# A hybrid attention and ConvGLU block: three more column pairs by seven products, remainders of the pair sums by accumulating transfers, and the row of 1/rms by way of DRAM

## The chip, the cores and the metric

One core of a Trainium2 chip runs the whole kernel. Its engines run side by side, each in its own order: TensorE (PE in the profile, its weight loads PEld), VectorE (DVE), ScalarE (ACT), GpSimd (POOL) and SyncE (SP). SP and POOL issue nearly all DMA transfers here, each from a queue that it works through in order. The metric is the device time of one execution in microseconds.

## The reference

One transformer-like layer on x of 512 rows (tokens) by 1024 columns, all in float32:

```
h    = rms_norm(x, norm1_g);  proj = h @ w_in          # q, k, v of branches A and B, gates gA, gB
yA   = chunked softmax attention(qA, kA, vA) @ w_branch_a
yB   = stick-breaking attention(qB, kB, vB) @ w_branch_b
x    = x + (sigmoid(gA) * yA + sigmoid(gB) * yB) @ w_out
hid  = rms_norm(x, norm2_g) @ w_ffn_up                 # 1024 -> 2 * 2816
gate, up = causal depthwise conv of width 3 (hid) + bias
x    = x + (silu(gate) * up) @ w_ffn_down              # 2816 -> 1024
```

rms_norm divides a row by the root of its mean square, so 1/rms is one number per token.

## The kernel before

Every float32 product is made of three products in the faster fp32r format. A matrix is split into hi (the value rounded to fp32r, a copy on ACT) and lo (value minus hi, a subtraction on DVE), and hi·hi, hi·lo and lo·hi are added up in PSUM.

The weights stream through in chunks. A chunk is loaded into one of two `raw` tiles by SP, split while TensorE works on the chunk before (`split_gen`), and then multiplied (`run_chunk`). The order of chunks is a fixed list: qA0, kA0, vA0, qA1, kA1, vA1, gA0, vB0, gA1, ..., then the output projections, then `up0` to `up21`, then the down projection in two sweeps of eleven chunks, `dn0_0` to `dn0_10` and `dn1_0` to `dn1_10`. Attention steps run between the chunks of the first half. A scheduler fixes the final order of the instructions on every engine when the program is built.

**The row of 1/rms.** 1/rms of the first norm is made as a column (one number per partition, `rstd`, in the tile `cols`). The gates gA and gB and the keys kB are computed with tokens along the free axis, so they need 1/rms as a row that is the same in all partitions, `rrow`. `norm1_row` makes it with four small TensorE products of `rstd` with the identity into a PSUM bank and a copy of that bank on ACT (L351 to L358). Its users are L514 (gA), L498 (kB) and L544 (gB).

**An up chunk** `up{j}` holds 128 columns of the gate and 128 of the up half. An ordinary one (`up_body`) takes two products of 8 x 3 matmuls with 512 columns. The chunks in the list `SEVEN` use Strassen's scheme of seven half-size products instead of eight: `up_seven` has seven products of 4 x 3 matmuls with 256 columns (L998), over sums of blocks of the weights (`block_sums`, tile `sx`, with their split in `wxh` and `wxl`) and over sums of blocks of the input (`token_sums`, four tiles with tag `ts`). Its results are put together on ACT and DVE in `pc`, `hg` and `hu`. After the products, `conv` applies the three taps (one ACT and two DVE instructions for each half), ACT takes the silu in the one buffer `cg`, and DVE multiplies into a slot of `ub`, which has four.

**A pair** is two neighbouring chunks, after odd j. The down projection uses a seven-product scheme as well, so `pair_sums` makes sums of blocks of the two results (tile `st`, one buffer) and splits them into hi and lo: `ax` (four blocks, used in the first sweep) and `ay` (three blocks, used in the second). `halves` does the split: a copy on ACT (L908) and a subtraction on DVE (L909) for each of four pieces of 768, 256, 256 and 512 columns. There are eight buffers with tag `ax` and one `ay`, so `ay` of pairs 0 to 6 is written to the DRAM tensor `ayd` by a DMA on POOL (L933), and `fetch` brings it back later (L953), into tiles that are free by then: the first five after `up18`, two more in the first down sweep. Pair 8 has its `ax` in a `ts` tile and its `ay` in `wxh`.

## Time and profile before

| | us |
|---|---|
| median of 3 runs | 726.53 (726.07 to 726.63) |
| the profiled execution | 726.66 |
| its span in the trace | 724.9 |
| TensorE busy in the span | 718.6 (99%) |
| VectorE busy | 565.4 (78%) |
| ScalarE busy | 401.5 (55%) |
| GpSimd busy | 53.6 (7%) |

The span reaches from the first to the last instruction; 1.8 us of the execution lie around it. The granted TensorE clock is 1.00 throughout. GpSimd's busy time leaves out the DMA issues, which its queue also holds.

### The profile page before, as it was taken

The numbers are of one execution on the slowest core, as the hardware profiler recorded it, in microseconds if no ns is written. First come the engines' busy times: TensorE is split into PE (matmuls) and PEld (weight loads), VectorE is DVE, ScalarE is ACT, GpSimd is POOL, SyncE is SP. The second block draws the span as 40 slices with busy tenths as digits, with TensorE's granted clock in tenths as the row PEclk, the third lists the DMA queues.
The fourth block names the chain that finished last, engine by engine and source line by source line (L and its number), as shares of the span: only waits on it lengthen the run. The fifth ranks groups of instructions, "written<-read, shape, count | busy, mean of one in ns | idle before, by whom it ended". The sixth has DMA issues, their size and how long they took to land.

```text
span 724.9 us, 10589 instructions
## 1 busy us (share of the span) xinstructions
PE 718.6 (99%) x4019; PEld 627.5 (87%) x4019; DVE 565.4 (78%) x1030; ACT 401.5 (55%) x727; POOL 53.6 (7%) x95
## 2 busy tenths in 40 slices
PE   8999999999999999999999999999999999999997
PEld 8999998888988888888889889889898988888886
DVE  6678867775988888566275799998979985997686
ACT  6675656657767676442254556655545653543541
POOL 2701200000101011000012000000000100000000
PEclk9999999999999999999999999999999999999999
DMA  8632232211313111314536613544335553564563
GB/s 308 250 131 78 83 117 74 74 59 58 118 63 113 59 59 59 136 68 144 195 149 239 203 62 156 186 135 160 118 145 186 181 184 117 173 243 174 177 222 116
DMA packets 24786, 100.91 MB, mean 139 GB/s; under 512 B 2592, under 2 KB 7328, under 8 KB 17184
## 3 DMA queue, kind: packets, MB, share of 16 engines
q1 hardware_dynamic: 21792, 87.00, 33.8%
q0 software_dynamic: 2656, 13.11, 5.0%
q8 instruction: 31, 0.51, 0.3%
q14 instruction: 19, 0.16, 0.1%
q10 hardware_dynamic: 288, 0.14, 0.1%
HBM read 88.44 MB, written 11.80 MB: 138 GB/s over the span
## 4 chain that ended last, share of the span: by engine, by line
PE 98%; DMA 1%; SPq 0%; DVE 0%; ACT 0%; DVEq 0%; issue 0%
PE P L1087 14%; PE p L998 7%; PE pg L254 4%; PE pg L253 4%; PE pg L255 4%; PE pu L254 4%; PE pu L255 4%; PE pu L253 4%; PE qkB L255 2%; PE gB L255 2%; PE qkB L253 2%; PE gA L253 2%; PE gA L254 2%; PE gB L253 2%; PE gA L255 2%; PE qkB L254 2%
## 5 line engine op out<-in xcount | busy, mean ns | idle before, releaser
L253 PE MATMUL pg<-hth,whi_up 128*128 128x512 f32 (+1 forms) x152 | 55.7, 367 | 0.0
L255 PE MATMUL pg<-hth,wlo_up 128*128 128x512 f32 (+1 forms) x152 | 55.7, 366 | 0.0
L254 PE MATMUL pg<-htl,whi_up 128*128 128x512 f32 (+1 forms) x152 | 55.7, 366 | 0.0
L254 PE MATMUL pu<-htl,whi_up 128*128 128x512 f32 (+1 forms) x152 | 55.6, 366 | 0.0
L253 PE MATMUL pu<-hth,whi_up 128*128 128x512 f32 (+1 forms) x152 | 55.6, 366 | 0.0
L255 PE MATMUL pu<-hth,wlo_up 128*128 128x512 f32 (+1 forms) x152 | 55.6, 365 | 0.0
L1087 PE MATMUL P<-whi_dn,ax 128*128 128x512 f32 x176 | 54.4, 389 | 0.0
L149 ACT CAST whi_dn<-raw_dn 128x1024 fp32r<-128x1024 f32 x33 | 34.3, 1051 | 25.5 <-PE P L1087 15.2
L145 DVE TENSOR_TENSOR wlo_dn<-raw_dn,whi_dn 128x1024 fp32r<-128x1024 f32 x33 | 40.0, 1224 | 9.2 <-ACT whi_dn L149 9.1
L228 DVE TENSOR_TENSOR wlo_up<-raw_up,whi_up 128x1024 fp32r<-128x1024 f32 (+1 forms) x40 | 41.2, 1062 | 7.0 <-ACT whi_up L226 7.0
L226 ACT CAST whi_up<-raw_up 128x1024 fp32r<-128x1024 f32 (+1 forms) x40 | 34.5, 917 | 14.7 <-PE pu L254 7.9
L1087 PE MATMUL P<-whi_dn,ay 128*128 128x512 f32 x132 | 40.8, 389 | 0.0
L1087 PEld LDWEIGHTS P<-whi_dn,ax 128*128 128x128 f32 x176 | 33.0, 188 | 6.8
L1087 PE MATMUL P<-wlo_dn,ax 128*128 128x512 f32 x88 | 34.2, 389 | 0.0
L254 PEld LDWEIGHTS pu<-htl,whi_up 128*128 128x128 f32 x152 | 28.6, 188 | 4.7
L253 PEld LDWEIGHTS pu<-hth,whi_up 128*128 128x128 f32 x152 | 28.5, 188 | 4.7
L255 PEld LDWEIGHTS pg<-hth,wlo_up 128*128 128x128 f32 x152 | 28.6, 188 | 4.7
L255 PEld LDWEIGHTS pu<-hth,wlo_up 128*128 128x128 f32 x152 | 28.5, 188 | 4.6
L253 PEld LDWEIGHTS pg<-hth,whi_up 128*128 128x128 f32 x152 | 28.6, 188 | 4.6
L254 PEld LDWEIGHTS pg<-htl,whi_up 128*128 128x128 f32 x152 | 28.6, 188 | 4.5
L633 DVE TENSOR_TENSOR_SCAN aB<-aB,reset 128x127 f32<-128x127 f32 (+3 forms) x32 | 26.0, 817 | 6.7 <-ACT aB L628 6.7
L1087 PEld LDWEIGHTS P<-whi_dn,ay 128*128 128x128 f32 x132 | 24.8, 188 | 5.1
(303 smaller groups left out, 2240.3 us busy)
## 6 DMA issues: line engine op xcount, KB each, us to landing
raw_up<-in_wts SPq DMA_DIRECT2D x22, 1024.0 KB, 4.8
raw_dn<-in_wd SPq DMA_DIRECT2D x11, 1024.0 KB, 4.8
raw_dn<-in_wd SPq DMA_DIRECT2D x11, 512.0 KB, 3.4
ayd<-ay POOLq DMA_DIRECT2D x7, 768.0 KB, 5.2
ay<-ayd POOLq DMA_DIRECT2D x7, 768.0 KB, 6.5
raw_gA<-in_wts SPq DMA_DIRECT2D x4, 1024.0 KB, 4.7
raw_qkB<-in_wts SPq DMA_DIRECT2D x4, 1024.0 KB, 4.8
raw_gB<-in_wts SPq DMA_DIRECT2D x4, 1024.0 KB, 4.7
```

Source lines behind the costliest of these rows:

```text
L145: chain("halves", V.tensor_tensor(o, x, y, op=op))
L149: chain("casts", A.copy(hi[:, sl], src))
L226: A.copy(hi[:, sl], raw[:, sl])
L228: E.tensor_tensor(lo[:, sl], raw[:, sl], hi[:, sl].bitcast(F32), op=ALU.subtract)
L253: PE.matmul(ps, sh, mh, start=first, stop=False)
L254: PE.matmul(ps, sh, ml, start=False, stop=False)
L255: PE.matmul(ps, sl, mh, start=False, stop=last)
L633: V.tensor_tensor_scan(ar, ar, reset[:, S - n:S - 1][:, ::-1], 1.0, op0=ALU.mult, op1=ALU.max)
L998: PE.matmul(ps, st, mv[:, k, :], start=first and k == 0 and n == 0, stop=last and k == 3 and n == 2, skip_group_check=True)
L1087: chain("products", PE.matmul(dst, st, mv, start=first and n == 0, stop=last and n == 2, skip_group_check=True))
```

## The change

- `SEVEN` grows from five chunks (5, 8, 11, 14, 17) to eight (5, 8, 10, 12, 14, 16, 18, 20), so that from up7 on every second chunk is of this kind.
- In `halves`, for pairs 0 to 8, lo is no longer a DVE subtraction. ACT writes minus the rounded value into lo (a second ACT instruction for each piece), and a DMA on POOL adds the value to it in place (`accum_op=ALU.add`). Pairs 9 and 10 keep the subtraction.
- Pair 8 gets an `ax` buffer and the `ay` buffer like the others. For this, `ay` of pair 7 is written to `ayd` too, and `ax` of pair 0 is written to a new DRAM tensor `axd` and fetched into a `ts` tile after `up20`.
- The fetches are emitted after `up20` (pairs 0 and 1) and after chosen down chunks (the others).
- `norm1_row` goes. SP writes `rstd` to a DRAM tensor `row` and later reads it back, spread over all partitions, into `rrow`; `behind(..., (late["ld"],))` places the write behind the load of vA1's weights in SP's queue, and the read behind that of vB0.

```diff
-SEVEN = (5, 8, 11, 14, 17)
+SEVEN = (5, 8, 10, 12, 14, 16, 18, 20)
...
-            SP.dma_start(raw[:, sl], wts[i, :, sl])
+            late["ld"] = SP.dma_start(raw[:, sl], wts[i, :, sl])
...
-    rrow = norm1_row()
     for s in range(len(steps)):
+        if s == 4:
+            behind(SP.dma_start(row.rearrange("t p -> p t"), rstd), (late["ld"],))
+        if s == 9:
+            behind(SP.dma_start(rrow, bass.AP(row.tensor, row.offset, [[0, P], [1, S]])), (late["ld"],))
...
                 A.copy(a[:, sl], src)
-                ins.append(V.tensor_tensor(a[:, n + o:n + sl.stop], src, a[:, sl].bitcast(F32), op=ALU.subtract))
+                if i < 9:
+                    A.activation(lo, src, AF.Copy, scale=-1.0)
+                    G.dma_start(lo, src, accum_op=ALU.add)
+                else:
+                    ins.append(V.tensor_tensor(lo, src, a[:, sl].bitcast(F32), op=ALU.subtract))
...
-            if j // 2 < 7:
+            if j // 2 < 8:
                 G.dma_start(ayd[j // 2], pairs[j // 2][1].bitcast(F32))
+            if j // 2 == 6:
+                G.dma_start(axd, pairs[0][0].bitcast(F32))
...
-        if j == 18:
-            for i in range(5):
+        if j == SEVEN[-1]:
+            keep[0] = fp.tile([P, S], F32, tag="hg", name="t2_0")
+            ax0 = fp.tile([P, 2048], F32R, tag="ts", name="ax0_", bufs=4)
+            G.dma_start(ax0, axd)
+            pairs[0] = (ax0, None)
+            for i in range(2):
                 fetch(i)
...
+            n = ({1: 2, 3: 6, 5: 7, 7: 3, 9: 4}, {0: 5})[s].get(i)
+            if n is not None:
+                fetch(n)
```

How the built order changes at the places that the prediction speaks of. First SP's queue in the first half, where `raw_` are weight loads and `tt` the bias tiles; before:

```order
L132 DMA raw_vA1_715<-in_wts 128x2048
L132 DMA raw_gA0_928<-in_wts 128x2048
L586 DMA tt2_880<-in_rbx 128x512
L586 DMA tt3_1132<-in_rbx 128x512
L132 DMA raw_vB0_1124<-in_wts 128x2048
L586 DMA tt4_1381<-in_rbx 128x512
```

and SP's queue at the same place now:

```order
L132 DMA raw_vA1_711<-in_wts 128x2048
L723 DMA row_192<-cols_191 128x4x1
L132 DMA raw_gA0_925<-in_wts 128x2048
L582 DMA tt2_877<-in_rbx 128x512
L582 DMA tt3_1130<-in_rbx 128x512
L132 DMA raw_vB0_1121<-in_wts 128x2048
L725 DMA rrow_193<-row_192 128x512
L582 DMA tt4_1379<-in_rbx 128x512
```

The two transfers stand where `behind` puts them; the loads around them keep their order.

Second, POOL's queue through the up chunks, from pair 3 to the fetches; before:

```order
L933 DMA ayd_108<-ay3_4972 128x1536
L933 DMA ayd_108<-ay4_5175 128x1536
L933 DMA ayd_108<-ay5_5383 128x1536
L953 DMA ay0_6036<-ayd_108 128x1536
L933 DMA ayd_108<-ay6_5544 128x1536
L953 DMA ay1_6038<-ayd_108 128x1536
```

and POOL's queue now, for one pair (pair 4, as for the others):

```order
L907 DMA ay4_5197<-ub_4182 128x256
L907 DMA ax4_5196<-st4_5198 128x256
L907 DMA ax4_5196<-ub_4182 128x768
L907 DMA ay4_5197<-st4_5198 128x512
L933 DMA ayd_108<-ay4_5197 128x1536
```

and now at the turn to the down projection, where one queue of fetches stands:

```order
L1061 DMA ax0__6389<-axd_109 128x2048
L956 DMA ay3_6790<-ayd_108 128x1536
L956 DMA ay4_6862<-ayd_108 128x1536
L956 DMA ay2_6557<-ayd_108 128x1536
L956 DMA ay1_6393<-ayd_108 128x1536
L956 DMA ay5_6935<-ayd_108 128x1536
```

Each write to `ayd` now stands behind four accumulating transfers and has to wait for the two into `ay`, and five fetches of `ay` stand together behind the one of `ax0_`.

Third, ACT from the end of up10 to the end of pair 4, now (L903 are the rounded copies, L906 the negated ones, L199 the split of up12, L850 the taps):

```order
L903 CAST ay4_5197<-ub_4182 128x256
L906 ACTIVATE ay4_5197<-ub_4182 128x256
L199 CAST wxh_up12_5354<-sx_up12_5271 128x512
L199 CAST whi_up12_5352<-raw_up12_5190 128x1024
L850 ACTIVATE cg10_5314<-hg10_5221,par_88 128x512
L199 CAST whi_up12_5352<-raw_up12_5190 128x1024
L903 CAST ax4_5196<-st4_5198 128x256
L906 ACTIVATE ax4_5196<-st4_5198 128x256
L903 CAST ax4_5196<-ub_4182 128x768
L906 ACTIVATE ax4_5196<-ub_4182 128x768
L850 ACTIVATE ub_4182<-hu10_5222,par_88 128x512
L903 CAST ay4_5197<-st4_5198 128x512
```

Here every rounded copy has a negated one right behind it; the negated copy of the last piece follows as the next row.

More of the change, by code (lines that the diff above doesn't have):

```diff
@@ L264, in block_kernel @@
     htd = dram.tile([NT, 2, P, S], F32, tag="htd", name="htd")
-    ayd = dram.tile([7, P, 1536], F32, tag="ayd", name="ayd")
+    ayd = dram.tile([8, P, 1536], F32, tag="ayd", name="ayd")
+    axd = dram.tile([P, 2048], F32, tag="axd", name="axd")
     reset = pool_c.tile([P, S], F32, tag="reset", name="reset")
@@ L349, in norm1 @@
         V.tensor_scalar_mul(nrstd[:, c], rstd[:, c], -1.0)
-    def norm1_row():
-        ps = PV("rrow")
-        for t in range(NT):
-            PE.matmul(ps[:, t * P:(t + 1) * P], rstd[:, t:t + 1].to_broadcast([P, P]), ident,
-                      start=True, stop=True)
-        r = pool_c.tile([P, S], F32, tag="rrow", name="rrow")
-        A.copy(r, ps)
-        return r
+    row = dram.tile([NT, P], F32, tag="row", name="row")
+    rrow = pool_c.tile([P, S], F32, tag="rrow", name="rrow")
     kg = par[:, C_KG:C_KG + 1]
@@ L875, in pair_sums @@
         t = {}
-        if i < 8:
+        if i < 9:
             ax = fp.tile([P, 2048], F32R, tag="ax", name=f"ax{i}", bufs=8)
             ay = fp.tile([P, 1536], F32R, tag="ay", name=f"ay{i}")
-        elif i == 8:
-            ax = fp.tile([P, 2048], F32R, tag="ts", name=f"ax{i}", bufs=4)
-            ay = fp.tile([P, 1600], F32R, tag="wxh", name=f"ay{i}")[:, 0:1536]
-            keep[0] = fp.tile([P, S], F32, tag="hg", name="t2_0")
         else:
@@ L907, in halves @@
                 sl = slice(o, o + src.shape[-1])
+                lo = a[:, n + o:n + sl.stop]
                 A.copy(a[:, sl], src)
-                ins.append(V.tensor_tensor(a[:, n + o:n + sl.stop], src, a[:, sl].bitcast(F32), op=ALU.subtract))
+                if i < 9:
+                    A.activation(lo, src, AF.Copy, scale=-1.0)
+                    G.dma_start(lo, src, accum_op=ALU.add)
+                else:
+                    ins.append(V.tensor_tensor(lo, src, a[:, sl].bitcast(F32), op=ALU.subtract))
             return ins
@@ L948, in fetch @@
     def fetch(i):
-        tag = {0: "sx", 1: "wxl"}.get(i, "ts" if i < 5 else "ax")
-        n, bufs = {"sx": (1536, 1), "wxl": (1600, 1), "ts": (2048, 4), "ax": (2048, 8)}[tag]
+        tag = {0: "sx", 1: "wxl", 2: "wxh"}.get(i, "ts" if i < 6 else "ax")
+        n, bufs = {"sx": (1536, 1), "wxl": (1600, 1), "wxh": (1600, 1), "ts": (2048, 4), "ax": (2048, 8)}[tag]
         ay = fp.tile([P, n], F32R, tag=tag, name=f"ay{i}", bufs=bufs)[:, 0:1536]
@@ L1174, in steps0 @@
             yield from late_pair(ss[i][:2])
-            fetch(i - 4)
     def steps1():
```

## The prediction

> **What bounds the kernel now.** I read the page's busy times first, then what TensorE waited for, then the chain that ended last, then busy times by stage.

> ```profile
> PE 718.6 (99%) x4019; PEld 627.5 (87%) x4019; DVE 565.4 (78%) x1030; ACT 401.5 (55%) x727; POOL 53.6 (7%) x95
> ...
> PE warm L301 <- DVE warm L298: 1.1, 1, 1.1
> PE qA L379 <- ACT whi_qA L226: 0.6, 1, 0.6
> PE qA L379 <- DVE whi_qA L224: 0.4, 1, 0.4
> ```

> The three waits are all that PE has, and they lie in the first microseconds. From there to the end it never stands still, so the time is the sum of what its matmuls take: whatever leaves PE's stream shortens the kernel by just that, until something makes PE wait. The chain of work that ended last has the prices (start, duration, matmuls):

> ```profile
> 435.60 9.89 PE p L998 x84
> 467.28 9.89 PE p L998 x84
> 615.78 104.94 PE P L1087 x462
> ```

> From the start of up5 to that of up8 are 31.68 us, for one seven-product chunk of 9.89 and two ordinary ones: (31.68 - 9.89) / 2 = 10.90 us for an ordinary chunk. The down projection runs through from 615.78 with no gap.

> The engines that feed PE have less room than the page's shares say (PE, PEld, DVE, ACT, POOL busy in each stretch):

> ```profile
> 435.60:467.28 31.68, 31.68 (x182) 27.92 (x182) 31.68 (x52) 20.01 (x32) 1.07 (x2) 1.00 0.47 176
> 467.28:498.96 31.68, 31.68 (x182) 27.92 (x182) 29.45 (x47) 17.37 (x27) 1.07 (x2) 1.00 0.42 150
> 530.64:562.32 31.68, 31.68 (x182) 27.92 (x182) 26.39 (x41) 16.88 (x26) 1.09 (x2) 1.00 0.49 169
> ```

> Each stretch is three up chunks. DVE is full in the first, and still 83% busy in the last; ACT is at 53 to 63%, the 16 DMA engines at 42 to 49%.

> **The change part by part. Three more seven-product chunks.** 3 x (10.90 - 9.89) = 3.0 us leave PE's stream. In exchange DVE gets work, priced by these rows (median of min/median/max, ns; the first four are the subtractions that the change takes away):

> ```profile
> L909 DVE TENSOR_TENSOR ay<-ub,ay x9: 416/422/439, 427.0 to 580.9; 128x256 fp32r<-128x256 f32 x9
> L909 DVE TENSOR_TENSOR ax<-st,ax x9: 412/419/433, 434.0 to 582.6; 128x256 fp32r<-128x256 f32 x9
> L909 DVE TENSOR_TENSOR ax<-ub,ax x9: 949/953/969, 435.2 to 583.3; 128x768 fp32r<-128x768 f32 x9
> L909 DVE TENSOR_TENSOR ay<-st,ay x9: 679/689/703, 437.4 to 587.7; 128x512 fp32r<-128x512 f32 x9
> ...
> L200 DVE TENSOR_TENSOR wxl_up<-sx_up,wxh_up 128x1024 fp32r<-128x1024 f32 x5 | 6.1, 1224 | 0.0
> ...
> 444.13 0.43 DVE L898 TENSOR_TENSOR st<-ub 128x256 f32<-128x256 f32 x1
> 444.46 0.43 DVE L909 TENSOR_TENSOR ay<-ub,ay 128x256 fp32r<-128x256 f32 x1
> ```

> The last two start 0.33 apart and take 0.43 each: back to back, an instruction costs about 0.1 less than its duration. An extra chunk of the seven adds four block sums of 512 columns (4 x 0.69), the split of the sums (1.22 + 0.69) and five combinations of 256 (5 x 0.42), 6.8 less 11 x 0.1, so 5.7 us; three chunks 17 us. **The accumulating transfers** take 0.42 + 0.42 + 0.95 + 0.69 less 4 x 0.1 = 2.1 us per pair off DVE, 19 us over nine pairs. DVE's sum is the same within 2 us. What changes is its density: from up7 on, a pair of chunks (10.90 + 9.89 = 20.8 us of PE) holds one of the seven, one ordinary chunk and one pair's four sums, some 29 instructions and 18 us by the same prices, or 87%, as now. DVE's queue stays under PE's, so I cost this at nothing; the cover is about 2.7 us per pair of chunks, and the split of the next weights would be late first if it goes.

> ACT gets the negated copies and the extra chunks' splits and copies:

> ```profile
> L908 ACT CAST ay<-ub x9: 390/407/417, 423.8 to 580.5; 128x256 fp32r<-128x256 f32 x9
> L908 ACT CAST ax<-st x9: 392/403/407, 428.3 to 581.5; 128x256 fp32r<-128x256 f32 x9
> L908 ACT CAST ax<-ub x9: 825/836/842, 430.2 to 581.8; 128x768 fp32r<-128x768 f32 x9
> L908 ACT CAST ay<-st x9: 604/622/645, 435.4 to 585.5; 128x512 fp32r<-128x512 f32 x9
> L199 ACT CAST whi_up<-raw_up x10: 1042/1048/1055, 425.7 to 552.2; 128x1024 fp32r<-128x1024 f32 x10
> L851 ACT ACTIVATE cg<-hg,par x5: 802/817/817, 454.3 to 573.0; 128x512 f32<-128x512 f32 x5
> ```

> A negated copy is not in the trace; I take the copy of the same size, 2.27 us a pair. In 20.8 us (a pair of chunks) that is 11 points more, and 1 or 2 for the denser chunks, on top of about 58%: 70%, hidden.

> **The new loop of waits.** `ay` has one buffer. Pair i+1's first copy into it waits for the write of pair i's `ay` to DRAM, which waits on POOL for the two accumulations into `ay`, which wait for the negated copies. By ACT's order above, from the first copy of a pair into `ay` to the last negated one stand the eight copies (4.5), one 512-column piece of the split (0.61), two of 1024 (2.1) and two taps (1.6): 8.8 less 13 x 0.1, so 7.5 us. Then the accumulation lands, then the write. The rows nearest to these two (times of landing, on the same queue: 256 KB to DRAM; then `ay` of 768 KB to DRAM and back; then the way back alone):

> ```profile
> L323 POOL DMA_DIRECT2D htd<-xf_n x8: 542/549/747, 376.9 to 392.4; - x8
> DMA to landing us min/median/max: 2.3/3.3/6.0
> ...
> L933 POOL DMA_DIRECT2D ayd<-ay x7: 533/533/542, 438.8 to 553.9; - x7
> L953 POOL DMA_DIRECT2D ay<-ayd x7: 530/539/554, 553.3 to 632.5; - x7
> DMA to landing us min/median/max: 3.5/5.3/9.0
> ...
> ay<-ayd POOLq DMA_DIRECT2D x7, 768.0 KB, 6.5
> ```

> An accumulation is nowhere in the trace. Its last piece is 256 KB, so from below 2.3, and from above 9.0, the worst landing of this queue; it comes right behind a 384 KB piece of its own kind, so I take 5.3. The loop is 7.5 + 5.3 + 5.3 = 18.1 us, and it has 20.8: hidden, by 2.7. With 9.0 it is 21.8 and PE's pace follows it. The sums' buffer `st` and the slots of `ub` are freed by the same landings, but are wanted again a whole pair of chunks later, so they hold longer than this loop. Four more issues of 0.53 us for each pair cost nothing on POOL, which has only the write beside them.

> [...]

> **The row of 1/rms.** PE's four products (eight rows) go:

> ```profile
> 29.27 1.06 PE L354 MATMUL rrow<-ident,cols 128*128 128x128 f32 x8
> 30.16 0.38 PE L469 MATMUL qkT_A<-ident,n_qA 128*128 128x128 f32 x2
> ...
> L514 DVE TENSOR_TENSOR mixA<-gA,rrow x8: 673/688/693, 93.0 to 185.3; 128x512 f32<-128x512 f32 x8
> ...
> 35.27 0.33 SPq L132 DMA_DIRECT2D raw_vA<-in_wts  x1
> 48.06 0.33 SPq L132 DMA_DIRECT2D raw_gA<-in_wts  x1
> ...
> 60.95 0.33 SPq L132 DMA_DIRECT2D raw_vB<-in_wts  x1
> 70.82 0.33 SPq L586 DMA_DIRECT2D tt<-in_rbx  x1
> ...
> tt<-in_rbx SPq DMA_DIRECT2D x8, 256.0 KB, 3.1
> ```

> The next work starts 0.89 us after them, so 0.9 us leave the stream. On SP the write comes after the load at 35.27, with 12.8 us before the next load; the read after 60.95, with 9.9 us before the next transfer. The write has 512 pieces of one number, which no row shows; it may take 25 us before the read would wait. The read is as large as a bias tile (3.1 us) and is first used at 93.0. Hidden on both sides, so the row is worth 0.9 us whole.

> **The turn to the down projection.** `ax0_` (1 MB) may start once up20 has read its tile, in its second product of seven: 5/7 x 9.89 + 10.90 = 18 us before dn0_0, against a worst landing of 9.0 for three quarters of the bytes. Right behind it five fetches start together, now one chunk before the down projection, where before four started four chunks ahead. What that does to a weight load stood at 578 (four fetches in flight, then the landing of the one load issued among them):

> ```profile
> ay<-ayd POOLq DMA_DIRECT2D x4, 768.0 KB, 7.7
> ...
> DMA to landing us min/median/max: 8.8/8.8/8.8
> ```

> A down chunk of the first sweep is 24 of the 462 matmuls, 104.94 x 24 / 462 = 5.45 us, and wants 1 MB. Three loads are issued ahead of the sweep, so a landing of 8.8 falls into their lead; I cost it at 0, at worst at two loads late by 3.4 us (8.8 - 5.45) each, so 0 to 7.

> **Sum.** 726.66 - 3.0 - 0.9 = 722.8 against the profiled execution; that lies 0.13 above the median of 726.53, so 722.6 for the median. Its own range is 721.7 (a seven-product chunk saving 0.2 more, the row 1.06 by its busy time) to 723.6 (one microsecond of small waits).

> **The rivals.**
> 1. *The accumulation loop becomes the bound* (slower). Place: ACT's first copy into `ay` of each pair waits for the write to `ayd`. It decides from a landing of 8.0 on (20.8 - 7.5 - 5.3), and costs 1 us for each further us at each of the seven turns from pair 1 to pair 8. At 13, twice the 6.5 of a fetch, that is 7 x 5 = 35 us: 757. At 9.0 it is 7, so 729.6. For it: one buffer, and a transfer with no row. Against: the medians of this queue are 3.3 and 5.3, and 9.0 is its worst.
> 2. *POOL's descriptors are held up by DVE* (slower). If each of the four issues waits out a DVE instruction of 1.2 us, the loop grows by 4.8 to 22.9, 2.1 over, seven times: 15 us, 737. Against: in the first stretch above DVE is 31.68 of 31.68 busy, and the writes issued there took the same 0.53 as all. [...]
> 3. *The crowded turn* makes dn0_1 or dn0_2 late: 722.6 + 2 to 4, say 725. For it: a landing of 8.8; against: the lead.
> 4. *DVE or ACT is late in the denser rhythm*: the chain through the one `cg` buffer now waits behind negated copies, and PE waits for split weights some 0.5 us in each of the seven pairs of chunks: 726, and the gain is gone. For it: DVE full at 435; against: 2.7 us of room, and DVE has less to do by then than before.

> **How the numbers follow.** A measurement of this kernel can tell about 0.2% (1.45 us) from no change: faster is below 725.1, slower above 728.0. The forecast 0.63; rival 1 0.13 and rival 2 0.03, both slower; rival 3 0.14, of which 0.10 stays faster; rival 4 0.07, of which 0.02 stays faster. Faster 0.63 + 0.10 + 0.02 = 0.75, slower 0.16, the same 0.09. The range from 721.7 to 728 takes in the forecast and rivals 3 and 4, and leaves out rivals 1 and 2 and little below.

> **What would show it.** PE busy lower by 3.9 us with no wait longer than the ones above; 672 matmuls at L998's successor in eight blocks of 9.89; no row of PE for `rrow`; DVE busy within 2 us of 565; ACT up by some 30 us; accumulations landing in 3 to 7 us, with ACT's first copy into `ay` not waiting for POOL's write. It would be wrong if PE waits for split weights in the up chunks in a rhythm of 20.8 us or more, if ACT or DVE waits on accumulations, or if the first down chunks wait for their loads.

## The result: 768 us, 5.7% slower

| | before | after |
|---|---|---|
| median, us | 726.3 (725.87 to 726.63) | 768.06 (764.88 to 768.82) |
| ratio | | 1.0567 (interval 1.0537 to 1.0597) |
| span of the profiled execution, us | 724.9 | 766.5 |

One of the eleven executions of the row alone (below) took 894.66 us at a granted clock of 0.754; its ratio leaves that one out.

The page of the changed kernel, at the places that were shown of before:

```profile
span 766.5 us, 10988 instructions
PE 729.7 (95%) x4119; PEld 637.7 (83%) x4119; DVE 565.6 (74%) x1027; ACT 423.3 (55%) x780; POOL 87.5 (11%) x135
```

Contrary to what stands above of the time before, GpSimd's busy time holds the DMA issues: 36 accumulations of some 0.86 us each are 31 us of its 87.5.

What TensorE waited for (total us, times, longest), now with up chunks at the top where there were none:

```profile
PE p L1001 <- ACT pc L1006: 12.2, 6, 3.9
PE p L1001 <- ACT whi_up L199: 8.9, 3, 5.5
PE pg L253 <- DVE hu L1016: 3.2, 1, 3.2
```

These name ACT and DVE, which are no busier than predicted. So the next question is what made those two late. The waits of the other engines answer it:

```profile
ACT ay L903 <- DMA ayd<-ay: 49.3, 7, 11.7
...
DVE st L892 <- DMA ay<-st: 21.3, 5, 5.2
```

At seven of the eight turns from one pair to the next, ACT stood at its first copy into `ay` until the write of the old `ay` to DRAM had landed. Five times DVE stood at the next pair's first sum until the accumulation that reads `st` had landed.

By stage (PE, PEld, DVE, ACT, POOL busy, then the granted clock; from the first seven-product chunk to the first down product, and from there to the end), after and then before:

```profile
435.90:652.90 217.00, 190.37 (x1105) 169.28 (x1104) 157.11 (x242) 119.38 (x198) 37.20 (x49) 0.94 0.61 173
652.90:766.50 113.60, 106.74 (x463) 86.01 (x461) 90.77 (x118) 46.67 (x59) 1.07 (x2) 1.00 0.56 199
```
```profile
435.40:615.60 180.20, 180.20 (x997) 157.64 (x996) 158.74 (x246) 99.48 (x150) 6.45 (x12) 1.00 0.44 157
615.60:724.90 109.30, 105.11 (x463) 86.47 (x461) 89.27 (x116) 45.90 (x57) 1.07 (x2) 1.00 0.52 183
```

The span grew by 41.6 us: 36.8 in the up chunks, 4.3 in the down projection, 0.5 ahead of both. In the up chunks PE idled 26.6 us. It was also *busy* 10.2 us longer although three chunks got shorter, because the clock granted to it fell to a mean of 0.94.

**What the chain looks like for one pair.** POOL's queue and ACT's row in the same stretch (start, duration; in brackets the idle time before):

```profile
550.24 0.86 POOL L907 DMA_DIRECT2D ax<-st  x1 [2.37 <-ACT ax L906]
556.46 0.88 POOL L907 DMA_DIRECT2D ax<-ub  x1 [5.36 <-DVE sx_up L179]
561.12 0.85 POOL L907 DMA_DIRECT2D ay<-st  x1 [3.79 <-issue]
568.81 0.56 POOL L933 DMA_DIRECT2D ayd<-ay  x1 [6.83 <-issue]
```
```profile
545.87 0.41 ACT L903 CAST ay<-ub 128x256 fp32r<-128x256 f32 x1 [6.09 <-DMA ayd<-ay]
...
552.40 0.63 ACT L906 ACTIVATE ay<-st 128x512 fp32r<-128x512 f32 x1
...
572.78 0.41 ACT L903 CAST ay<-ub 128x256 fp32r<-128x256 f32 x1 [8.03 <-DMA ayd<-ay]
```

ACT had all its negated copies of the pair done at 553.0. Yet the accumulation into the last piece was issued at 561.12. The times from issue to landing, of the four POOL rows in order, show why:

```profile
DMA to landing us min/median/max: 5.9/5.9/5.9
DMA to landing us min/median/max: 4.3/4.3/4.3
DMA to landing us min/median/max: 7.1/7.1/7.1
DMA to landing us min/median/max: 3.9/3.9/3.9
```

550.24 + 5.9 = 556.1, and the next issue is at 556.46. 556.46 + 4.3 = 560.8, and the next is at 561.12. Each accumulation is issued about 0.3 us behind the landing of the one before: only one is open (issued and not yet landed) at a time. In the same kernel, at none of the 36 accumulations was another one still open at its issue. That this queue can hold more shows in the kernel before, where the fetches (plain transfers) go out three in a row, and the fourth starts when the first has landed (572.82 + 5.2 against 578.29):

```profile
572.82 1.61 POOL L953 DMA_DIRECT2D ay<-ayd  x3 [18.37 <-PE p L998]
578.29 0.54 POOL L953 DMA_DIRECT2D ay<-ayd  x1 [3.86 <-PE pg L255]
```

So the theory ahead of the experiments (theory Q) was: POOL's queue has room for three plain transfers or for one accumulation, the four accumulations of a pair queue behind each other's landings, and the one buffer `ay` turns that queue into the pace of the kernel. It gave 722 to 728 us for a queue with twice the room, and 722 to 735 for plain copies in place of the accumulations. In this pair the loop from copy to copy is 572.78 - 545.87 = 26.9 us; the eight writes of `ayd` start at 450.8 to 619.1, a mean of 24.0 us apart, where PE needs 20.8.

### The profile page after: what moved, and what is told of

Read it like the earlier page. It is cut to its first block, busy times and chain, and to the rows that moved or that the text cites. A ratio compares the mean times of both kernels' runs of the same rounds, so it can differ in the third digit from the quotient of the medians.

```text
span 766.5 us, 10988 instructions
## 1 busy us (share of the span) xinstructions
PE 729.7 (95%) x4119; PEld 637.7 (83%) x4119; DVE 565.6 (74%) x1027; ACT 423.3 (55%) x780; POOL 87.5 (11%) x135
## 5 line engine op out<-in xcount | busy, mean ns | idle before, releaser
L253 PE MATMUL pg<-hth,whi_up 128*128 128x512 f32 (+1 forms) x128 | 47.8, 373 | 3.2 <-DVE hu L1016 3.2
L254 PE MATMUL pg<-htl,whi_up 128*128 128x512 f32 (+1 forms) x128 | 47.4, 370 | 0.0
L255 PE MATMUL pg<-hth,wlo_up 128*128 128x512 f32 (+1 forms) x128 | 47.3, 370 | 0.0
L254 PE MATMUL pu<-htl,whi_up 128*128 128x512 f32 (+1 forms) x128 | 46.3, 362 | 0.0
L253 PE MATMUL pu<-hth,whi_up 128*128 128x512 f32 (+1 forms) x128 | 46.3, 362 | 0.0
L255 PE MATMUL pu<-hth,wlo_up 128*128 128x512 f32 (+1 forms) x128 | 46.2, 361 | 0.0
L1001 PE MATMUL p<-hth,whi_up 128*128 128x256 f32 x64 | 20.5, 321 | 21.1 <-ACT pc L1006 12.2
L228 DVE TENSOR_TENSOR wlo_up<-raw_up,whi_up 128x1024 fp32r<-128x1024 f32 (+1 forms) x34 | 34.0, 1029 | 3.0 <-ACT whi_up L226 3.0
L903 ACT CAST ay<-ub 128x256 fp32r<-128x256 f32 x11 | 4.5, 406 | 54.3 <-DMA ayd<-ay 49.3
L1001 PEld LDWEIGHTS p<-hth,whi_up 128*128 128x128 f32 x64 | 13.5, 211 | 23.9 <-ACT pc L1006 13.6
L226 ACT CAST whi_up<-raw_up 128x1024 fp32r<-128x1024 f32 (+1 forms) x34 | 28.4, 891 | 7.0 <-issue 3.6
L631 POOL TENSOR_SCALAR_AFFINE_SELECT bB<-bB 128x128 f32<-128x128 f32 x32 | 13.5, 428 | 152.8 <-DVE bB L630 146.6
## 6 DMA issues: line engine op xcount, KB each, us to landing
ayd<-ay POOLq DMA_DIRECT2D x8, 768.0 KB, 4.3
ay<-ayd POOLq DMA_DIRECT2D x8, 768.0 KB, 7.1
```

The source lines that it names most:

```text
L226: A.copy(hi[:, sl], raw[:, sl])
L228: E.tensor_tensor(lo[:, sl], raw[:, sl], hi[:, sl].bitcast(F32), op=ALU.subtract)
L253: PE.matmul(ps, sh, mh, start=first, stop=False)
L254: PE.matmul(ps, sh, ml, start=False, stop=False)
L255: PE.matmul(ps, sl, mh, start=False, stop=last)
L631: G.affine_select(b[:, n - P:n], b[:, n - P:n], pattern=[[-1, P]], compare_op=ALU.is_gt, fill=0.0, base=0, channel_multiplier=1)
```

## The experiments

All are edits of the changed kernel unless said otherwise; the ratios are to the kernel before, which ran beside each (725.9 to 726.0 us).

**Room in the queue.** The kernel is built with a setting of 512 bytes (`dynamic_dma_scratch_size`) for POOL's transfers, which the change didn't touch.

```diff
-    nc = bacc.Bacc("TRN2", ..., dynamic_dma_scratch_size=512)
+    nc = bacc.Bacc("TRN2", ..., dynamic_dma_scratch_size=1024)
```

> The changed kernel with the ring of descriptors for POOL's transfers twice as large (dynamic_dma_scratch_size 1024 for 512); the built order of every engine is the same. [...] Theory A (addition): the adding itself is slow, whatever the ring; landings stay at 3 to 7 us each and the time above 750. Theory D (density): DVE and ACT are late with eight chunks of the seven; the time stays at 768.

Measured: 736.03 us (733.29 to 740.42), ratio 1.0142 (1.0101 to 1.0183). The instructions on every engine stand in the same order, so 32 of the 42 us are the room in the queue alone. The time lies above the 722 to 728 of theory Q and below the 750 of theory A: the room is the larger part of the loss and not all of it. Up to three accumulations are open now (1.5 and 1.8 us apart):

```profile
528.33 0.84 POOL L907 DMA_DIRECT2D ax<-st  x1 [2.35 <-ACT ax L906]
529.80 0.88 POOL L907 DMA_DIRECT2D ax<-ub  x1 [0.63 <-ACT ax L906]
531.57 0.85 POOL L907 DMA_DIRECT2D ay<-st  x1 [0.89 <-ACT ay L906]
```

and of ACT's 49.3 us behind the write little is left:

```profile
ACT ay L903 <- DMA ayd<-ay: 7.1, 2, 4.1
```

**The same transfers without the addition.** This kernel leaves the addition out: lo then holds the plain value. Still 512 bytes.

```diff
-                    G.dma_start(lo, src, accum_op=ALU.add)
+                    G.dma_start(lo, src)
```

> The changed kernel, whose 36 accumulating transfers are plain copies of the same pieces (the addition is left out, so lo holds the value itself). The built order is the same. [...] Theory A: no addition, so 722 to 735 as well, but with each landing much shorter than 3 to 7 us even for the last of three in flight. Theory D: 768.

Measured: 726.89 us (725.51 to 733.48), ratio 1.0018 (0.9998 to 1.0038), span 723.9. Same order, same number of POOL issues, same ACT work: everything that the change lost goes with the addition. That is what theories Q and A both gave, since a plain copy takes less room as well; theory D falls. Its stages are also the cleanest measure of the rest of the change:

```profile
435.90:613.70 177.80, 177.47 (x1106) 160.26 (x1105) 156.47 (x243) 119.88 (x199) 26.07 (x49) 1.00 0.65 218
613.70:723.90 110.20, 105.67 (x463) 86.28 (x461) 90.64 (x118) 47.12 (x59) 1.07 (x2) 1.00 0.53 189
```

The up chunks' busy time fell from 180.20 to 177.47, so the three sevens bring 2.7 us; 0.3 of it is idle again, the down projection takes 0.9 more, and the first half 0.5. What reaches the span is 1.0 us in this execution, which is 1.3 us faster than the median of the ten; by the medians nothing is gained.

**The subtraction back on DVE**, with eight sevens and the row by DRAM.

```diff
-                if i < 9:
+                if i < 0:
```

> The changed kernel with the remainders of pairs 0 to 8 by DVE's subtraction again; the eight chunks of the seven, the buffers and fetches of pairs 0, 7 and 8, and the row by way of DRAM stay. Theories Q and A: no accumulation, so no loop through POOL; DVE has 20.2 us of work in 20.8 us of PE for a pair of chunks (97%), so 723 if that is enough and up to 740 if DVE falls behind. Theory D: above 750.

Measured: 730.15 us (728.82 to 732.04), ratio 1.0049 (1.0032 to 1.0066); DVE busy 581.8. Its largest waits beside those of the start are 2.8 us of PE on DVE at the turn to the down projection and 0.9 on ACT's `pc` in the up chunks. So the denser rhythm does need something off DVE: with half of the subtractions taken off it, 725.33 us were measured (below, with 1280 bytes).

**The accumulations with the old five sevens.**

```diff
-SEVEN = (5, 8, 10, 12, 14, 16, 18, 20)
+SEVEN = (5, 8, 11, 14, 17)
```

> The changed kernel with the old list of five chunks of the seven (the accumulations, the buffers and the row stay; the fetches come after up17). Theories Q and A: the loop through POOL takes 24 us and more against 20.8 to 21.8 us of PE for a pair of chunks, so 740 to 760. Theory D: DVE and ACT have more room than before, so 725.8 (726.7 less 0.9 for the row).

Measured: 765.0 us (763.53 to 766.23), ratio 1.0534 (1.0519 to 1.055), with the same wait on ACT:

```profile
ACT ay L903 <- DMA ayd<-ay: 49.5, 6, 11.5
```

That is above the 740 to 760 expected of the queue, and far from the 725.8 of theory D. 39 of the 42 us are there without the three extra sevens, and the intervals of the two kernels overlap.

**How many fit.** 768 bytes, as a count of the theory, by which two accumulations may be open:

```diff
-    nc = bacc.Bacc("TRN2", ..., dynamic_dma_scratch_size=512)
+    nc = bacc.Bacc("TRN2", ..., dynamic_dma_scratch_size=768)
```

> The changed kernel with 768 bytes for the POOL queue's descriptors. [...] 512 gave one, 1024 three, 1280 four. Time between 736 and 768, about 738 to 750, since half of the queueing goes.

Measured: 738.51 us (733.56 to 739.99), ratio 1.0158 (1.0132 to 1.0184). They go in twos: the third of these waits for the first (532.86 + 7.5 = 540.4, then the issue).

```profile
532.86 0.86 POOL L907 DMA_DIRECT2D ax<-st  x1 [2.33 <-ACT ax L906]
534.36 0.85 POOL L907 DMA_DIRECT2D ax<-ub  x1 [0.64 <-ACT ax L906]
540.69 0.87 POOL L907 DMA_DIRECT2D ay<-st  x1 [5.48 <-ACT whi_up L226]
```

The time is at the lower edge of what was expected. Two places already bring nearly all that three bring (736.03 us, and the intervals overlap).

**1280 bytes** in place of the 512, and nothing else.

```diff
-    nc = bacc.Bacc("TRN2", ..., dynamic_dma_scratch_size=512)
+    nc = bacc.Bacc("TRN2", ..., dynamic_dma_scratch_size=1280)
```

> [...] With 1024 three accumulations went out 1.5 us apart and the fourth of a pair still waited for a landing; 736.0 us. Theory Q (the queue's memory counts out how many transfers may be open, and an accumulation takes about twice a plain transfer's share): four fit, the fourth is issued 1.5 us behind the third, and what is left beyond the plain copies' 726.9 us shrinks from 9 us to 1 to 4: 727 to 731. Rival L (what is left is the accumulation's own landing, 7 to 10 us when several are open against 2 to 6 for plain copies): four open at once land no sooner than three, 734 to 738.

Measured: 736.36 us (734.86 to 739.41), ratio 1.0151 (1.0133 to 1.0169): no better than 1024, as the rival had it. Four can be open now, which happened at one of the nine pairs; that pair with 1280 and then with 1024 bytes, where the fourth waited:

```profile
466.04 0.86 POOL L907 DMA_DIRECT2D ax<-st  x1 [5.59 <-ACT ax L906]
466.65 1.13 POOL L907 DMA_DIRECT2D ay<-ub  x1
468.12 0.84 POOL L907 DMA_DIRECT2D ax<-ub  x1 [0.34 <-ACT ax L906]
469.17 0.84 POOL L907 DMA_DIRECT2D ay<-st  x1 [0.20 <-issue]
477.43 0.56 POOL L933 DMA_DIRECT2D ayd<-ay  x1 [7.42 <-issue]
```
```profile
463.18 0.84 POOL L907 DMA_DIRECT2D ax<-st  x1 [5.50 <-ACT ax L906]
...
465.26 0.85 POOL L907 DMA_DIRECT2D ax<-ub  x1 [0.35 <-ACT ax L906]
470.34 0.84 POOL L907 DMA_DIRECT2D ay<-st  x1 [4.22 <-ACT whi_up L226]
474.44 0.56 POOL L933 DMA_DIRECT2D ayd<-ay  x1 [3.27 <-issue]
```

The write follows the first issue by 11.4 us with four open and by 11.3 with three. In that pair, what the fourth gained at its issue it lost in its landing; over all pairs its median landing is 7.9 us here and 7.3 with 1024, against 5.7 as a plain copy.

A part of what is left shows in this trace. ACT's waits behind the write are down to 3.4 us, but PE has a gap of 2.41 us that goes back to the one buffer `st`: DVE stands until the accumulation that reads it has landed, and `hu`, which comes next in DVE's order, is late for PE:

```profile
447.99 0.43 DVE L892 TENSOR_TENSOR st<-ub 128x256 f32<-128x256 f32 x1 [4.08 <-DMA ay<-st]
448.80 0.80 PE L253 MATMUL pg<-hth,whi_up 128*128 128x512 f32 x1 [2.41 <-DVE hu L1016]
```

PE's other long gap in the up chunks, 3.1 us at 608.4, goes back through DVE to a weight load of the down projection that took 8.35 us to land.

**Accumulating into `ax` only.** What is left of the loss with 1280 bytes is either the loop of `ay` or the accumulations as such.

```diff
-                if i < 9:
+                if i < 9 and n == 1024:      # ax; the pieces of ay are subtracted on DVE
...
-    nc = bacc.Bacc("TRN2", ..., dynamic_dma_scratch_size=512)
+    nc = bacc.Bacc("TRN2", ..., dynamic_dma_scratch_size=1280)
```

> The run with 1280 bytes, but only the two pieces of ax are made by accumulating transfers; the two of ay go back to a copy on ACT and a subtraction on DVE. So the write of ay to DRAM waits for no accumulation of its own pair's ay, only for its place in POOL's queue. DVE gets 2 of the 4 subtractions of each pair back (half or a little less of the 16 us between 565.6 and 581.8). If what is left of the loss is the loop of ay (copy, accumulation, write, next copy), this is below the run with 1280 bytes and near the plain copies' 726.9 (725.5 to 728); if DVE's load decides (all four subtractions on DVE gave 730.2), it lies at 728 to 730.

Measured: 725.33 us (724.22 to 726.89), ratio 0.9991 (0.9982 to 0.9999). The ten microseconds are gone, with DVE at 571.7, and this is the one version that lies below the kernel before, by less than the 0.2% that I had called a difference. That the rest goes with the accumulations into `ay` is shown; whether they cost it by the loop of its write, by holding `st`, or by the number of open transfers isn't, since this kernel also has half as many accumulations.

**The same with 512 bytes.**

```diff
-    nc = bacc.Bacc("TRN2", ..., dynamic_dma_scratch_size=1280)
+    nc = bacc.Bacc("TRN2", ..., dynamic_dma_scratch_size=512)
```

> The two accumulations of ax alone, as in the last run, but with 512 bytes for the POOL queue's descriptors, as in the changed kernel. Theory (the loss is the queue's one place times the loop of ay): now the write of ay waits for one accumulation's landing ahead of it on POOL's queue (from the run before: ax<-st issued 567.73, +5.92; then ax<-ub, +5.06; then the write, +3.56: about 583 against the next copy at 585.1 on ACT), so the loop of 20.8 us still closes with 2 us to spare and it takes 725.5 to 728. Rival (one transfer in flight costs by itself, the loop of ay or not): POOL late as in the changed kernel, 735 or more.

Measured: 731.53 us (727.38 to 732.59), ratio 1.0062 (1.0042 to 1.0082): between the two expectations, so a miss of both. The loop closes except at one place, where the write of `ax` of pair 0 to DRAM takes its turn first and ACT waits 8.41 us for the write of `ay` behind it; PE's gaps beyond the start are small (1.6 us at most) and many, and I can't put all of the 6 us at one of them.

**The row alone**, in the kernel before. The lines that define `norm1_row` and `late` change as in the change and aren't shown.

```diff
...
-    rrow = norm1_row()
     for s in range(len(steps)):
+        if s == 4:
+            behind(SP.dma_start(row.rearrange("t p -> p t"), rstd), (late["ld"],))
+        if s == 9:
+            behind(SP.dma_start(rrow, bass.AP(row.tensor, row.offset, [[0, P], [1, S]])), (late["ld"],))
```

> The kernel before with one part of the change only: the row of 1/rms goes by DRAM (write in step 4, read in step 9, behind the loads), the eight products of 128x128 on PE and ACT's copy of the result are gone; five seven-chunks and the subtraction on DVE as before. The prediction's theory: the products' 0.9 us were on PE's path, so 725.0 us (ratio 0.9988). Rival (from the changed kernel's trace, where the first half ended at 379.4 us against 378.9): PE had to wait at that place for ACT's qA weights anyway and the gap in front of them grows by what the products took, so 725.7 to 726.5 (ratio 0.9995 to 1.0007).

Measured: 726.03 us, ratio 1.0004 (0.9995 to 1.0013). A gain of 0.9 us (0.9988) is outside the interval.

**The row made on PE again**, with 1280 bytes, and then in the version that accumulates into `ax` only:

```diff
...
+    rrow = norm1_row()
     for s in range(len(steps)):
-        if s == 4:
-            behind(SP.dma_start(row.rearrange("t p -> p t"), rstd), (late["ld"],))
-        if s == 9:
-            behind(SP.dma_start(rrow, bass.AP(row.tensor, row.offset, [[0, P], [1, S]])), (late["ld"],))
```

> The run with 1280 bytes, with the row of 1/rms again made by eight products on PE: the seven-chunks and the accumulations without the row. If the row by DRAM is worth 0.9 us, this is 0.9 us above that run; if it is worth nothing or costs (first half 0.5 us later in the changed kernel), this is the same or up to 1 us below it.

Measured: 736.0 us (732.47 to 740.5), ratio 1.0142 (1.011 to 1.0173), against 1.0151 with the row by DRAM.

> The run with the accumulations of ax alone and 1280 bytes (725.33 us), with the row of 1/rms made on PE as in the kernel before. The row by DRAM alone measured 1.0004 (0.9995 to 1.0013), so this is within 0.5 us of 725.33; were the row worth the prediction's 0.9 us, 726.2.

Measured: 726.31 us (724.37 to 729.86), ratio 1.0002 (0.9989 to 1.0016). That is the figure of the theory that gives the row 0.9 us, but the two intervals overlap (0.9982 to 0.9999 with the row by DRAM), so this pair of runs doesn't settle it. The run of the row alone has the narrower interval, and I go by it.

## Why the prediction was wrong, step by step

**The loop of `ay`: the step that failed.** The prediction's sum was 7.5 + 5.3 + 5.3 = 18.1 us against 20.8. In the pair shown, ACT's stretch took 553.0 - 545.9 = 7.1, so that term was right for this pair. The write and the step to the next copy took 572.78 - 568.81 = 4.0, below its 5.3. The last accumulation landed in 7.1, with a median of 4.7 over the nine, inside the 2.3 to 9.0 that I had bounded. What was missing is a fourth term, 561.1 - 553.0 = 8.1 us between the last negated copy and the issue of the last accumulation, in which POOL waited for two earlier landings. In the eight pairs this fourth term is 6.0 to 11.2 us (and ACT's stretch 1.8 to 11.5). The step reads "Four more issues of 0.53 us for each pair cost nothing on POOL, which has only the write beside them": I had costed the issues and not the queue's capacity. The rows of the crowded fetches could have told me: the prediction calls them "four fetches in flight", but three went out together, and the fourth only when the first had landed, so at most three were open.

**Rival 1, the loop as the bound,** was right in place and sign, and wrong in its condition. It put the turning point at one landing of 8.0 us; every size's median landing was below 5 us, but a pair's landings come one after the other. Its price of 1 us per turn for each us over 20.8 gives (24.0 - 20.8) x 7 = 22 us for the measured mean period. PE idled 30.5 us more over the whole span, and the clock cost another 11 to 13 (below). I gave this rival 0.13.

**The buffer `st`** was said to "hold longer than this loop". DVE waited for it five times, 21.3 us in all: the queue delays its release as well.

**Rival 2, issues held up by DVE, falls.** An accumulation's issue takes the same in all 9 cases, at whatever DVE was doing:

```profile
L907 POOL DMA_DIRECT2D ax<-ub x9: 845/857/877, 433.4 to 632.2; - x9
```

That is 0.86 us and not the 0.53 of a plain one, and over all four pieces the longest is 0.91. With more room two of the 36 take 1.13 us with 1280 bytes, but the one shown above starts before the issue ahead of it has ended (466.65 against 466.04 + 0.86).

**Rival 4, the denser rhythm, falls as the cause** (five sevens cost nearly the same). Its "for", DVE's load, does show once the subtractions are back: 730.2.

**Rival 3, the crowded turn, holds in part.** The chain that ended last runs through a late load in the first down sweep, and the down projection takes 4.3 us longer, inside the prediction's "0 to 7", of which it took 0:

```profile
653.10 10.17 DMA raw_dn<-in_wd
```

With accumulating transfers out of the way (the plain copies) the same turn costs 0.9.

**The three sevens** were put at 3.0 us; 2.7 us of PE's busy time left in the up chunks (plain copies). Right. Over the whole span PE's busy time fell by 2.5 us and not by the 3.9 that the prediction named as a sign.

**DVE within 2 us of 565, ACT up by some 30:** 565.6, right; ACT rose by 21.8, since the negated copies were priced well but the total was put too high.

**The row of 1/rms: no gain found.** The products did leave PE, and their 0.9 us didn't leave the kernel: the first half ends at 379.4 us after, 378.9 before. A part of it turns up as waits that weren't there. Of the plain copies:

```profile
123.54 0.39 PE L591 MATMUL s_A<-skh_A,sq_A 128*128 128x256 f32 x1 [0.32 <-DVE st L599]
```

This 0.32 us, with 0.14 right after it, stands in the traces of the changed kernel and of its variants with the row by DRAM, and not in those with it on PE: the scheduler laid DVE's order out anew around the later row. The rest lies in the first ten microseconds, where PE's wait for the first qA weights was 0.96 us before and 0.9 to 2.4 in the other traces, with the row on PE as well; which of that is the change and which the run I can't tell.

## What to carry to other kernels

POOL's DMA queue had a capacity here (with 512 bytes three plain transfers or one accumulation) as well as an issue cost (0.53 us for a plain one before, 0.86 for an accumulation): count how many transfers of each kind it holds open, and look for it where issues stand one landing apart. An accumulating transfer took 1.5 to 2.5 times the room of a plain one (by the bounds below), so "four more cheap issues" behind a single buffer can turn into four landings in a row. In a kernel whose PE never idles, price a gap above its own length: each of the five gaps of 3.2 to 5.5 us in the up chunks of the changed kernel came with 3.4 or 6.8 us at half clock.

## What the runs showed of the hardware that I had not expected

**An addition alone costs little.** Landings of the changed kernel, where one is open at a time, and then of the plain copies (KB each, median us; the 256 KB piece of these lands in 5.7, behind others):

```profile
ax<-ub POOLq DMA_DIRECT2D x9, 384.0 KB, 4.3
ay<-st POOLq DMA_DIRECT2D x9, 256.0 KB, 4.7
...
ay<-ub POOLq DMA_DIRECT2D x9, 128.0 KB, 2.7
ax<-st POOLq DMA_DIRECT2D x9, 128.0 KB, 3.4
```
```profile
ax<-ub POOLq DMA_DIRECT2D x9, 384.0 KB, 3.1
...
ay<-ub POOLq DMA_DIRECT2D x9, 128.0 KB, 2.0
ax<-st POOLq DMA_DIRECT2D x9, 128.0 KB, 2.0
```

The addition adds 0.7 to 1.4 us to the medians of these three. None of them doubles (4.3 against 3.1, 2.7 against 2.0, 3.4 against 2.0). From 128 to 384 KB a plain landing grows by 1.1 us.

**A gap in PE's work also costs clock.** Behind PE's gap of 5.53 us that ended at 503.5 (columns as in the stages above):

```profile
506.00:508.00 2.00, 2.00 (x11) 2.00 (x11) 1.86 (x3) 0.00 (x0) 0.00 (x0) 0.50 1.04 222
508.00:510.00 2.00, 2.00 (x19) 2.00 (x19) 1.06 (x3) 1.82 (x3) 0.85 (x1) 0.96 0.94 384
```

The clock is halved until 508.2, for over 4 us, and that costs over 2 us of work. In this trace it happened behind the gaps of 3.2, 5.5, 3.9, 3.3 and 3.2 us, and not behind those of 1.75 us and less, five times in all. In the up chunks PE is busy 190.37 us here and 177.47 in the plain copies with the same matmuls, so 12.9 us went that way.

A gap's length alone doesn't decide it. With 1280 bytes the clock was halved from 448.8 to 452.2 behind the gap of 2.41 us shown above; with five sevens PE stood for 2.75 us until 449.5 and went on at full clock. The five half-clock stretches of the changed kernel begin at 450.1, 501.3, 559.4, 586.7 and 627.6 us and last 3.4 or 6.8 us, and the distances between their beginnings are 15, 17, 8 and 12 times 3.41 us: the clock changed on a raster of 3.41 us here. Counted back in steps of 3.41 us from each run's own first half clock (448.8 and 482.2), the 2.41 us lie in one stretch, and the 2.75 us in two, 1.3 and 1.4 us in each. That is a difference between the two, worked out as an estimate; from what gap on the clock is halved was not shown.
